# A streaming gradient: stores on their own DMA queue, loads issued one by one

## The chip, the cores and the metric

The kernel runs on one core of a Trainium2 chip. The metric is the device time of one execution in microseconds (us), taken as the median of several runs. Durations inside the kernel come from one profiled execution, recorded by the hardware profiler.

## The reference

```python
def setup_inputs():
    return {"x": np.random.randn(8192, 8192).astype(np.float32)}

def reference(x):
    return np.gradient(x, axis=1)
```

Along each row of 8192 numbers, an inner element of the result is half the difference of its two neighbours, `(x[j+1] - x[j-1]) / 2`; the first and last are the one-sided differences `x[1] - x[0]` and `x[8191] - x[8190]`. Input and output are 268.44 MB each, and there is nothing to reuse between rows.

## The kernel before

**Tiles.** The 8192 rows are cut into 32 sets of 256 rows. In a set each of the 128 partitions holds two whole rows side by side (`R = 2`), so a partition's piece is 16,384 numbers, 65,536 bytes, in one contiguous run of memory. Sets 0 to 2 are *plain*: partition p holds row pair p of the set. All others are *dealt*: the row pairs are given out to the partitions as cards are, so that partition 4a + q holds row pair 32q + a. Load and store of a set use the same order; the result of the computation does not depend on it.

**Slots.** Three buffers (`slot0` to `slot2`, `NB = 3`) take the sets in turn; set i uses slot i mod 3. A slot is 64 elements wider than a set. The load writes it from element 64 on (`SH = 64`), and VectorE writes the halved differences to the same buffer from element 1 on, in place but shifted, so that it overwrites only what it has already read.

**A set's work.** First GpSimd (POOL) computes the four one-sided differences per partition into `ends` (line 73). Then one custom VectorE (DVE) instruction does all the halved differences of the set, across the border between the two rows as well (line 79). Then the four end values are copied from `ends` over the wrong ones (line 90), by POOL in 12 of the sets and by DVE in the other 20. Then the store is issued (line 63). TensorE and ScalarE (ACT) do no work.

**Order.** All is written out by hand under `tc.manual_schedule()`. `chain` names for each step what it has to wait for: the end differences for the load, DVE for the end differences, the copy for DVE, the store for the copy, and load i for store i - 3, which empties its slot. Both loads (line 59) and stores (line 63) are issued by SyncE (SP), so they share one DMA queue, and its order is that of the program: three loads, three stores, three loads, three stores and so on, with two and two at the end. After the store of every third set come the loads of the next three:

```python
            if i % NB == NB - 1:
                for k in range(i + 1, min(i + 1 + NB, nsets)):
                    load(k)
```

Of the kernel before, what the change touches and what calls it, by code (L numbers as in the profile page):

```python
# [1 line left out]

# [4 lines left out]


@with_exitstack
def kernel(  # L10
    ctx: ExitStack,
    tc: tile.TileContext,
    x: bass.AP,
    out: bass.AP,
):

    nc = tc.nc
    P = nc.NUM_PARTITIONS
    n, m = x.shape
    R = 2  # L20
    NB = 3
    SH = 64
    W = R * m
    nsets = n // (P * R)
    f32 = x.dtype

    Q = 4

    def sets(t):

        plain = t.rearrange("(s p t) m -> s p (t m)", p=P, t=R)
        dealt = t.rearrange("(s q a t) m -> s a q (t m)", q=Q, a=P // Q, t=R)
        return [plain[i] if i < NB else dealt[i] for i in range(nsets)]

    x_sets, out_sets = sets(x), sets(out)

    pool = ctx.enter_context(tc.tile_pool(name="pool", bufs=1))
    edge = 256 // 4
    nends = nsets * R * 2
    ends_pad = pool.tile([P, nends + edge // 2], f32, name="ends", tag="ends")  # L40
    ends = ends_pad[:, 0:nends].rearrange("p (s t e) -> p s t e", t=R, e=2)
    slots = [pool.tile([P, SH + W], f32, name=f"slot{k}", tag=f"slot{k}") for k in range(NB)]
    loads, stores = [], [None] * nsets
    in_front = {}

    def chain(i, ins, *needed):

        group, engine = f"slot{i % NB}", ins.ins.engine
        keep = [o.ins for o in needed]
        if in_front.get(engine, (None,))[0] == group:  # L50
            keep.append(in_front[engine][1])
        tc.declare_no_dep(ins.ins, group=group, keep=keep, reason="implied by the needed step")
        tc.add_to_no_dep_group(group, ins.ins)
        in_front[engine] = group, ins.ins
        return ins

    def load(i):
        b = slots[i % NB]
        ins = nc.sync.dma_start(out=b[:, SH : SH + W], in_=x_sets[i])  # L59
        loads.append(chain(i, ins, *([stores[i - NB]] if i >= NB else [])))  # L60

    def store(i, done):
        ins = nc.sync.dma_start(out=out_sets[i], in_=slots[i % NB][:, 0:W])
        stores[i] = chain(i, ins, done)

    with tc.manual_schedule():
        for i in range(NB):
            load(i)
        for i in range(nsets):
            b = slots[i % NB]  # L70
            xin = b[:, SH : SH + W].rearrange("p (t m) -> p t m", m=m)

            ins = nc.gpsimd.tensor_sub(  # L73
                out=ends[:, i, :, :],
                in0=xin[:, :, 1 : m : m - 2],
                in1=xin[:, :, 0 : m - 1 : m - 2],
            )
            at = [chain(i, ins, loads[i])]
            ins = nc.vector._custom_dve(  # L79
                dve_ops.TENSOR_TENSOR_REDUCE_SUB_MAX,  # L80
                out=b[:, 1 : W - 1],
                in0=b[:, SH + 2 : SH + W],
                in1=b[:, SH : SH + W - 2],
                s0=0.0,
                s1=0.5,
            )
            halved = chain(i, ins, *at)
            res = b[:, 0:W].rearrange("p (t m) -> p t m", m=m)
            placer = nc.gpsimd if i % 5 in (1, 3) and i < nsets - 2 else nc.vector
            ins = placer.tensor_copy(out=res[:, :, 0 : m : m - 1], in_=ends[:, i, :, :])  # L90
            placed = chain(i, ins, halved)
            store(i, placed)
            if i % NB == NB - 1:
                for k in range(i + 1, min(i + 1 + NB, nsets)):
                    load(k)


# [1 line left out]
_INS = ['x']  # L99
_OUTS = [((8192, 8192), 'float32')]  # L100


# [23 lines left out]
```

## Time and profile before

| | |
|---|---|
| median of 3 runs | 1245.82 us (1245.79 to 1246.45) |
| the profiled execution | 1245.77 us, with a span of 1243.8 us |
| VectorE busy | 554.6 us (45%), 32 large instructions of 17.224 us each |
| GpSimd busy | 8.9 us (1%) |
| DMA | 536.88 MB on one queue, mean 432 GB/s, 9217 packets |
| loads, issue to landing | 32, median 57.9 us |
| stores, issue to landing | 32, median 40.3 us |

The span is the time from the first to the last recorded work of the profiled execution; its own time is 2.0 us longer. Engine rows give busy time and its share of the span. The slices of the page divide the span into 40 equal parts. A DMA row counts the packets that 16 DMA engines moved: 64 transfers, each with 128 packets of data (one for each partition) and 16 small ones that count the completion. "Issue to landing" runs from the issue of a transfer by SP until its last completion arrives, and so includes the time that it stands in the queue behind earlier transfers. SPq is the sequencer of SP that issues the transfers.

### The profile page before, as it was taken

To read this page: it belongs to the slowest core of one execution; us is meant where nothing else is said; L and a number is where in the kernel's file an instruction comes from. 1 tells how busy PE (TensorE), PEld (TensorE's weight loads), DVE (VectorE), ACT (ScalarE), POOL (GpSimd) and SP (SyncE) were. 2 spreads that over 40 slices of the span, in tenths; PEclk is the share of its full clock that TensorE was granted. 3 is DMA by queue.
4 is the path that set the end of the run, shared out by engine and by line. 5 is a ranking of instruction groups with operands and counts; after the bars stand their busy time and mean duration, and the time that the engine had idled before them with its cause. 6 is when DMAs were issued, how large, how long until landed. Compare 5 with 4: busy or idle time off the path is not lost.

```text
span 1243.8 us, 237 instructions
## 1 busy us (share of the span) xinstructions
DVE 554.6 (45%) x52; POOL 8.9 (1%) x48
## 2 busy tenths in 40 slices
DVE  2850583079009702850582079009603840591082
POOL 0000000000000000000000000000000000000000
DMA  9999999999999999999999999999999999999999
GB/s 405 438 438 424 419 438 438 438 438 426 434 430 430 438 438 438 426 438 432 430 432 438 438 430 434 438 432 430 432 438 434 434 434 438 432 430 430 436 409 405
DMA packets 9217, 536.88 MB, mean 432 GB/s; under 512 B 1024, under 2 KB 1024, under 8 KB 1024
## 3 DMA queue, kind: packets, MB, share of 16 engines
q1 hardware_dynamic: 9216, 536.88, 99.8%
q14 instruction: 1, 0.01, 0.0%
HBM read 268.44 MB, written 268.44 MB: 432 GB/s over the span
## 4 chain that ended last, share of the span: by engine, by line
another core or an unknown queue 74%; DVE 18%; DMA 3%; issue 2%; POOL 1%; SPq 0%; POOLq 0%
DVE slot L79 18%; DMA slot<-in_x_dram 3%; POOL ends L73 0%; POOL slot L90 0%; SPq L59 0%; POOLq L121 0%; DVE slot L90 0%
## 5 line engine op out<-in xcount | busy, mean ns | idle before, releaser
L79 DVE CUSTOM_DVE_ANT_0 slot<-slot 128x16382 f32<-128x16382 f32 x32 | 551.2, 17224 | 666.6 <-POOL ends L73 666.6
L73 POOL TENSOR_TENSOR ends<-slot 128x4 f32<-128x4 f32 x32 | 6.4, 200 | 987.4 <-DMA slot<-in_x_dram 987.4
L90 POOL COPY slot<-ends 128x4 f32<-128x4 f32 x12 | 2.3, 191 | 207.9 <-DVE slot L79 207.9
L90 DVE COPY slot<-ends 128x4 f32<-128x4 f32 x20 | 3.4, 172 | 0.7
L110 POOL MEMSET const-bfloat16-1.0<- 128x1 bf16 x1 | 0.1, 102 | 0.0
L110 POOL MEMSET const-uint8-127<- 128x1 uint8 x1 | 0.1, 102 | 0.0
L110 POOL MEMSET const-float32-0.0<- 128x1 f32 x1 | 0.1, 99 | 0.2 <-issue 0.2
L110 POOL MEMSET const-float32-1.0<- 128x1 f32 x1 | 0.1, 99 | 0.0
## 6 DMA issues: line engine op xcount, KB each, us to landing
slot<-in_x_dram SPq DMA_DIRECT2D x32, 57.9
out_dram<-slot SPq DMA_DIRECT2D x32, 40.3
```

Of the source, the lines that this page charges most:

```text
L73: ins = nc.gpsimd.tensor_sub(out=ends[:, i, :, :], in0=xin[:, :, 1 : m : m - 2], in1=xin[:, :, 0 : m - 1 : m - 2],)
L79: ins = nc.vector._custom_dve(dve_ops.TENSOR_TENSOR_REDUCE_SUB_MAX, out=b[:, 1 : W - 1], in0=b[:, SH + 2 : SH + W], in1=b[:, SH : SH + W - 2],
L90: ins = placer.tensor_copy(out=res[:, :, 0 : m : m - 1], in_=ends[:, i, :, :])
L110: nc = _bacc.Bacc("TRN2", target_bir_lowering=False, num_devices=1)
```

## The change

The stores are issued by ScalarE (`nc.scalar`) and so stand in a DMA queue of their own. The loads stay on SP. The load of set i + 3 is written right behind the store of set i, instead of three loads together behind every third store; its wait, for the store that empties its slot, is the same. Tiles, slots, layout and the computation are as before.

```diff
     def store(i, done):
-        ins = nc.sync.dma_start(out=out_sets[i], in_=slots[i % NB][:, 0:W])
+        ins = nc.scalar.dma_start(out=out_sets[i], in_=slots[i % NB][:, 0:W])
         stores[i] = chain(i, ins, done)
...
             store(i, placed)
-            if i % NB == NB - 1:
-                for k in range(i + 1, min(i + 1 + NB, nsets)):
-                    load(k)
+            if i + NB < nsets:
+                load(i + NB)
```

## The prediction

> **What bounds the kernel now.** I read the page's engine table and its slices first, then the DMA queues, then windows inside single phases, then the queue's own waits and the end of the chain.
>
> ```profile
> span 1243.8 us, 237 instructions
> ...
> DVE 554.6 (45%) x52; POOL 8.9 (1%) x48
> ...
> DMA  9999999999999999999999999999999999999999
> GB/s 405 438 438 424 419 438 438 438 438 426 434 430 430 438 438 438 426 438 432 430 432 438 438 430 434 438 432 430 432 438 434 434 434 438 432 430 430 436 409 405
> ...
> q1 hardware_dynamic: 9216, 536.88, 99.8%
> ```
>
> No slice has the DMA engines under nine tenths, and their one queue fills 99.8% of them; VectorE works 45% of the span. The kernel is bound by its transfers, so the question is whether the same bytes go through the 16 engines any slower or faster in another order. The windows, with columns DVE busy, POOL busy, granted TensorE clock, DMA share and GB/s, put one phase of stores and loads (80 to 138) beside one of loads and their computation (138 to 196) and the stores after it:
>
> ```profile
> 80.00:138.00 58.00, 0.00 (x0) 0.00 (x0) 1.00 1.00 434
> 138.00:196.00 58.00, 51.86 (x5) 0.79 (x4) 1.00 1.00 434
> 196.00:254.00 58.00, 0.15 (x1) 0.00 (x0) 1.00 1.00 434
> ```
>
> The rate is 434 GB/s whether VectorE works or not, and in both directions. The packet records say why: a packet of 65,536 B, one partition's row, takes 2,418 ns in 7,870 of 8,192 records and never under 2,415. Each engine moves 512 of them, 512 x 2.418 = 1,238.0 us. That is the floor, and the span is 5.8 us above it. For the slowest engine the 5.8 are: 1.8 until the first packet starts, 0.7 lost in the first packets, 1.0 where the first loads turn to the first stores (57 to 61 us), 1.6 over the other 20 turns and at the end, 0.8 after the last landing (rounded).
>
> ```profile
> SPq L63 <- DVE slot L90: 520.3, 20, 55.7
> SPq L59 <- DMA out_dram<-slot: 366.3, 29, 19.0
> SPq L63 <- POOL slot L90: 296.5, 12, 36.5
> ```
>
> These are the waits of SP's own queue. They are long, but they cost nothing: while SP waits for a store to land, two more stores are already queued on the engines.
>
> **What goes and what comes.** The profiled run took 1,245.77 us, its span 1,243.8; 2.0 lie outside the span and stay. The median of the runs is 1,245.82, so one more 0.05 is nothing.
>
> *Issue.* 32 stores leave SP for ACT, which has no other work. An issue takes 0.59 us on its sequencer (32 x 0.59 = 19 us per queue), all beside running transfers: 0. SP's load i+3 now waits for store i with no store behind it on SP; ACT's store i waits for set i's last copy, with only later stores behind it, which need later sets. DVE and POOL keep their order, in which POOL's end differences for set i+1 stand behind its copy for set i in 12 sets. Sets now arrive every 2 x 19.34 = 38.7 us, and landing to store issue takes 17.7 (22.69 to 40.38), so that wait is over 21 us before the next set lands: 0. The loads and stores still take turns on eight completion semaphores, but each user's predecessor is four sets older in its own direction, long landed: 0.
>
> *Do the engines ever run dry?* Stepping it through: loads 0 and 1 land as before; store 0 is issued at 40.4 and shares the engines with load 2, both done near 80. Store 1 has been queued since 59.5. Load 3 is issued at the landing of store 0 (in the present trace that takes 0.01 us at 81.6) and its first packet follows 1.0 us later (0.73 to 1.76 for load 0); for that long the load side is empty and store 1 has the engines alone. From then on one load and one store share, 38.7 us for each pair; every next store is issued 17.7 us after its load landed, so it stands ready 21 us early. Engines dry: 0. If that cover were gone, 29 reloads would each cost that 1.0 us and the landing's skew of up to 2.6 us, which is the rival below.
>
> *The end.* Now:
>
> ```profile
> 1184.91 0.20 POOL L73 TENSOR_TENSOR ends<-slot 128x4 f32<-128x4 f32 x1 [77.07 <-DMA slot<-in_x_dram]
> ...
> 1202.60 19.89 SPq L63 DMA_DIRECT2D out_dram<-slot  x2
> 1204.21 0.20 POOL L73 TENSOR_TENSOR ends<-slot 128x4 f32<-128x4 f32 x1 [19.10 <-DMA slot<-in_x_dram]
> ```
>
> Store 30 is issued at 1202.60 and needs 1.0 us to start; the slowest engine ends load 31 at 1204.14, so 0.3 is lost on it (it lands store 30 19.6 us later, not 19.3). After the change store 30 is ready long before: -0.3. But store 30 has then had the engines to itself about 1 us ahead of load 31, has 18.3 us left when load 31 lands, and store 31 starts 17.7 + 1.0 = 18.7 us after that landing: +0.4.
>
> *Turns.* This is the term that decides. The 21 turns between directions fall away: 1.3 of the 1.6 us is saved; the first turn's 1.0 stays, since loads still meet stores for the first time in the plain sets. In exchange load and store packets alternate on every engine. No second data queue exists in this trace, so the price of one alternation has to be bounded by the turns that it does show. Averaged over the 16 engines, the packets around a turn from loads to stores take too long by 984 ns at the first, then 140, 184, 84, 98, 0, 11, 7, 53 and 80; stores to loads 19, 5, 53, 0, 17, 4, 0, 5, 11 and 0. Early on the 16 engines turn within 0.5 us of each other, later within 1.6 to 2.6 us. Under two queues their turns are scattered, so the late ones are nearest: 30 + 6 = 36 ns for a pair from 580 us on. The bounds: 0 (three of the five last pairs are at 4 to 12 ns), and 84 ns, the mean over all but the first. Packets alternate from store 0's start to load 31's end, about 240 pairs per engine: 240 x 36 ns = +8.6 us, between 0 and 20.2.
>
> Here two rules of the skill bear. The Trainium skill, "DMA: Bandwidth & Descriptors", section "Queues, rings and completion order", says that an engine changes between queues only at packet boundaries, and that a packet typically holds 9 to 17 descriptors. A transfer here is 9,216 / 64 / 16 = 9 records per engine, so by that rule a whole transfer might be one turn: some 30 pairs, 30 x 84 = 2.5 us at the dearer price; no run here shows it yet. The same page of the Trainium skill, "Latency and other measured facts", gives 214 GB/s per direction as the full rate of a copy issued on the sync and scalar queues; by an estimate from that figure 536.88 MB / 428 GB/s = 1,254 us, which speaks against this change, while this trace's one queue shows 434.
>
> **Sum.** 1,243.8 - 1.3 - 0.3 + 0.4 + 8.6 = 1,251.2, and 2.0 outside: 1,253.2 us, slower by 0.6%.
>
> **Rivals.** A measurement of this kernel can tell about 0.2%, 2.5 us, from no change; slower begins at 1,248.3. With -1.2 from the other terms that takes 3.7 us in 240 pairs: 15 ns a pair.
>
> *No price for alternating (not slower).* The mechanism is that an engine fetches the next packet, of whichever queue, while it drains the present one. For it: three of the last five pairs below 15 ns, and 2,418 ns in all phases, so the engine and not the memory sets the rate. Against it: 64 and 80 ns in the two other pairs, and that no turn before 500 us was free in the direction load to store. Time: 1,253.2 - 8.6 = 1,244.6; with turns by whole transfers 1,247.1. It decides below 15 ns a pair.
>
> *Faster by over 0.2%.* The slowest engine has only 2.6 us to give (1.0 + 1.6): 1,243.2, which needs a free first turn, no price at all and no gap at the end. More would need packets under 2,418 ns, loads and stores overlapping inside an engine; no record is under 2,415 even at turns.
>
> *Lasting contention.* If reads and writes side by side in memory cost every packet what they cost in the first turns of the dealt sets (mean of 140, 184, 84 and of 19, 5, 53: 136 + 26 = 162 ns a pair), 240 x 162 = 39 us: 1,283. Against it: the price fell as the engines drifted apart.
>
> *The queues run dry.* If one queue took most of the engines, a store could end before the next is ready: up to 29 x (1.0 + 2.6) = 104 us, some 50 at half of it, 1,295. Against it: 21 us of slack.
>
> *The change doesn't do what it says.* SP's loads could still queue behind something. The order on each engine shows loads alone on SP and stores alone on ACT: no chance of its own.
>
> **Chances.** Alternation at 15 to 84 ns a pair 0.43 (1,248.3 to 1,264.8), lasting contention 0.05, dry queues 0.03: slower 0.51. No price, or whole transfers 0.42: same. Faster 0.07. Both signs hold much, so the likeliest case's own range is 1,248 to 1,265. The whole range is 1,243 to 1,268: from the slowest engine's full gain to a little past the dearest late price, leaving out the two dear rivals and half of faster.
>
> **What would show it.** Right: two hardware queues of 268 MB each; DMA share still at 99% or more; packets of loads and stores spread above 2,418 ns by some 18 ns on average; windows of 58 us at about 431 GB/s instead of 434; DVE waiting about 21 us for each set, evenly. If packets stay at 2,418 and the share at 99.8%, alternation is free and I am wrong by the 8.6. If packets exceed 2,500 throughout, it is contention. If the DMA share drops below 98%, a queue ran dry; POOL's waits for loads would then name it. If packets fall below 2,415, the floor was not one.

## The result and the profile after

The changed kernel is slower: 12 runs between 1,248.72 and 1,276.78 us, beside 1,245.42 to 1,246.80 for the kernel before. The ratio of the times is 1.0085, with a 95% interval of 1.0062 to 1.0108, or 1,256.4 us against 1,245.86. That ratio takes the eight runs within 1.5% of the fastest and leaves out four of 1,269 to 1,277 us, with which the median of the twelve is 1,261.6. The spread is a result by itself: 28 us where the kernel before has 1.4.

The profiled run took 1,250.96 us. These are the page's totals, slices and queues of the kernel after:

```profile
span 1248.6 us, 264 instructions
...
DVE 554.6 (44%) x52; POOL 8.9 (1%) x48
...
DMA  9999999999999999999999999999999999999997
GB/s 403 435 437 437 437 435 422 424 433 435 437 433 430 435 437 437 437 437 437 430 428 428 437 430 435 435 437 437 437 437 437 437 437 428 424 435 433 433 435 319
...
q1 hardware_dynamic: 4608, 268.44, 49.8%
q10 hardware_dynamic: 4608, 268.44, 49.6%
```

There are two queues of 268 MB now, and the engines are as busy as before in all slices but the last, where the rate drops to 319 GB/s. The windows of the kernel after (columns DVE busy, POOL busy, granted TensorE clock, DMA share, GB/s) put the middle beside the end:

```profile
600.00:658.00 58.00, 25.94 (x3) 0.39 (x2) 1.00 1.01 436
1100.00:1158.00 58.00, 28.32 (x3) 0.39 (x2) 1.00 1.00 435
1206.00:1228.00 22.00, 17.40 (x2) 0.20 (x1) 1.00 0.76 331
1228.00:1249.00 21.00, 0.00 (x0) 0.00 (x0) 1.00 0.83 359
```

Loads and stores mixed run at 435 GB/s, no less than in phases. The loss lies at 1,206 to 1,228 us, while VectorE computes the last set. In the kernel before the engines were full while it did (a window counts whole packets, so its share can pass 1.00):

```profile
1206.00:1222.00 16.00, 15.84 (x2) 0.00 (x0) 1.00 1.06 459
```

SP issues only loads now, and its waits are for the stores that empty their slots:

```profile
SPq L59 <- DMA out_dram<-slot: 1143.6, 29, 80.2
```

The end of the timeline of the kernel after gives the times:

```profile
1170.38 0.20 POOL L73 TENSOR_TENSOR ends<-slot 128x4 f32<-128x4 f32 x1 [38.18 <-DMA slot<-in_x_dram]
...
1208.98 0.20 POOL L73 TENSOR_TENSOR ends<-slot 128x4 f32<-128x4 f32 x1 [38.41 <-DMA slot<-in_x_dram]
1209.22 17.22 DVE L79 CUSTOM_DVE_ANT_0 slot<-slot 128x16382 f32<-128x16382 f32 x1 [21.18 <-POOL ends L73]
1226.48 0.17 DVE L90 COPY slot<-ends 128x4 f32<-128x4 f32 x1
```

Load 31 has landed on all engines at 1,208.9 us, 4.8 later than before (1,204.1), and its store can be issued at 1,226.7 only. By the packet records store 30 is over at 1,221.9 on the median engine and 1,223.4 on the last.

**An account for each run.** Linking each packet to the one that starts as it ends splits the records into 16 engines. A packet starts 4 ns ahead of its predecessor's recorded end, so 512 packets take 512 x 2.414 = 1,236.0 us. What lies between the first packet and the last beyond that is either the slowest engine's gaps in the last 100 us or time lost in slow packets. (The gap is the smallest over the engines. Where slow packets overlap, a few links go to the wrong engine; the sums here do not hang on that.) For the runs with packets of 32,768 B the floor is 1,024 x 1.209 = 1,238.0.

```
                first to last   lost by the     gap at      spread of the
                   packet      slowest engine   the end   landings of load 31
before            1240.9            4.9           0.1            2.5
after             1245.6            4.8           4.8            2.6
again_a           1267.0           26.2           4.9           20.0
again_b           1255.6           14.8           4.9           14.4
again_c           1255.5           14.7           4.8           17.3
swapped           1262.4           21.6           4.8           18.0
plain_all         1250.1           12.0           2.1            7.3
half              1249.5            8.7           4.9            6.5
hold_s30          1242.3            4.4           2.0            1.8
r1_two            1242.0            4.0           0.0       2.1 (last load)
r1_two_nb3        1246.2            4.5           3.7       1.8 (last load)
r1_one            1243.2            5.2           0.0       2.5 (last load)
```

The last column is the time from the first to the last of the 16 engines' landings, in us. In the first profile after, the gap at the end is the whole difference. In the longer runs one engine loses 10 to 21 us more.

### The profile page after: what moved, and what is told of

The parts are those of the page before. It is cut to its first block, busy times and chain, and to the rows that moved or that the text cites. A ratio compares the mean times of both kernels' runs of the same rounds, so it can differ in the third digit from the quotient of the medians.

```text
span 1248.6 us, 264 instructions
## 1 busy us (share of the span) xinstructions
DVE 554.6 (44%) x52; POOL 8.9 (1%) x48
## 2 busy tenths in 40 slices
DMA packets 9216, 536.88 MB, mean 430 GB/s; under 512 B 1024, under 2 KB 1024, under 8 KB 1024
## 4 chain that ended last, share of the span: by engine, by line
another core or an unknown queue 82%; DMA 9%; issue 3%; DVE 3%; SPq 1%; POOL 0%; POOLq 0%
DMA slot<-in_x_dram 5%; DMA out_dram<-slot 3%; DVE slot L79 3%; SPq L59 1%; POOL ends L73 0%; DVE slot L90 0%; POOLq L120 0%
```

## The experiments

**The kernel again, and the end by itself.** `again_a`, `again_b` and, on another occasion, `again_c` are the changed kernel unaltered.

> The changed kernel once more, unaltered, since its runs lie between 1248.7 and 1276.8 us while those of before lie within 1.4 us. Theory E (the end): the profile of after shows 8,192 packets at 2,418 ns almost throughout and a gap of some 5.7 us between the last packets of store 30 and the first of store 31; the runs differ in how far the stores lead the loads when load 31 lands, so a longer run has a longer gap there, 0.4 to some 20 us, and its middle stays at 434 GB/s. Theory C (contention): in a longer run the packets in the middle take longer, 20 us of excess being 40 ns per packet, a mean of about 2,458 ns instead of 2,423, and the gap at the end stays near 5.7 us. Theory D (dry queues): the DMA share of windows in the middle falls to 0.98 with packets at 2,418.

> The changed kernel unaltered a third time, for one more profile. Theory E: span less 1,242.9 us equals the gap between stores 30 and 31, packets at 2,418 ns. Theory C: the gap stays at 5.7 us and the excess of the packets over 2,418 ns, summed and divided by 16 engines, makes up the rest. Theory D: share in the middle below 0.985.

Measured: `again_a` 1,263.0 to 1,276.5 us (4 runs, median 1,269.1, ratio 1.0189, 1.0145 to 1.0233; the profile's span 1,269.9), `again_b` 1,260.5 (span 1,258.6). The gap on the slowest engine is 4.9 us in both, so theory E does not explain the spread. Theory C fails as written, too: the mean packets of `again_b` are 2,434 ns for loads and 2,418 for stores, an excess of 8 ns over all, 4 us per engine, while the span is 10 us longer than that of the first profile. The excess sits on one or two engines. Over 2,418 ns a packet, fourteen of the sixteen engines of `again_b` lost 2 to 6 us each, the other two about 14; those two land store 30 at 1,233.1 and 1,233.4 us, the others by 1,225.7. The windows of `again_a` show what that does at the end:

```profile
1100.00:1158.00 58.00, 24.19 (x2) 0.58 (x3) 1.00 0.99 416
1212.00:1231.00 19.00, 0.40 (x1) 0.20 (x1) 1.00 0.90 390
1231.00:1250.00 19.00, 16.99 (x2) 0.00 (x0) 1.00 0.17 72
1250.00:1270.00 20.00, 0.00 (x0) 0.00 (x0) 1.00 0.85 367
```

From 1,231 to 1,250 us nearly all engines stand still (share 0.17). Fifteen have ended store 30 and wait for the last set, which could not be computed before the straggler's share of load 31 had landed. From 1,100 to 1,158 us of this run, at 416 GB/s, the lag is about 20 us, nearly the 21 us by which a store is ready early. From 900 to 1,200 us the stores' packets average 2,486 to 2,513 ns, and 56% of all time lost in packets is in first packets of stores. That would fit a store queue that now and then runs dry as a consequence of the lag, but theory D is not shown by it: the share is 0.99, not 0.98, and from 100 to 1,200 us no engine stands idle for more than 2.6 us in all.

```diff
+    def sides(i):
...
+            if i < nsets - 1:
+                at = [sides(i)]
+            else:
+                at = [last_sides]
...
-            placer = nc.gpsimd if i % 5 in (1, 3) and i < nsets - 2 else nc.vector
+            if i == nsets - 2:
+                last_sides = sides(nsets - 1)
+            placer = nc.gpsimd if (i % 5 in (1, 3) and i < nsets - 2) or i == nsets - 2 else nc.vector
```

`sides(i)` issues the end differences of set i. Those of set 31 now stand ahead of set 30's copy, both on GpSimd.

> The changed kernel, but store 30 is held until load 31 has landed: GpSimd takes the end differences of set 31 ahead of the copy that releases store 30. Nothing else moves. Theory E: load 31 no longer shares the engines with store 30, lands some 4 us earlier, and store 30 covers the computation of set 31 in full; the gap ahead of store 31 falls from 5.7 to under 1 us, a gap of 1 to 3 us comes instead between load 31 and store 30, and the profiled span falls by 2 to 4 us against a run of the changed kernel with the same middle; if the end makes the spread, the runs also draw together, to within 3 us. Theory C: the gap at the end falls likewise, but the runs still spread over more than 10 us.

The timeline of `hold_s30` at the end, with POOL's differences of set 31 at 1,203.65 (`sides`) and the issues of stores 30 and 31, the first at 1,204.01, the second done 17.88 us later:

```profile
1203.65 0.20 POOL L68 TENSOR_TENSOR ends<-slot 128x4 f32<-128x4 f32 x1 [33.57 <-DMA slot<-in_x_dram]
...
1204.01 17.88 ACTq L63 DMA_DIRECT2D out_dram<-slot  x2
1221.14 0.17 DVE L97 COPY slot<-ends 128x4 f32<-128x4 f32 x1
```

Two windows of `hold_s30` show the engines before store 30 and beside it, while VectorE computes the last set:

```profile
1196.00:1206.00 10.00, 2.11 (x1) 0.32 (x2) 1.00 0.76 328
1206.00:1225.00 19.00, 15.28 (x2) 0.00 (x0) 1.00 1.02 442
```

Load 31 lands 5.3 us earlier than in the profile after, the gap ahead of store 31 is gone, one of 2.0 stands between load 31 and store 30, and the span is 1,245.3 instead of 1,248.6: 3.3 us less, where theory E names 2 to 4. Still the ten runs reach from 1,246.1 to 1,267.3 (ratio 1.0054, 1.0025 to 1.0083). The gap and the straggler are two losses.

**The order alone, on one queue.**

```diff
-        ins = nc.scalar.dma_start(out=out_sets[i], in_=slots[i % NB][:, 0:W])
+        ins = nc.sync.dma_start(out=out_sets[i], in_=slots[i % NB][:, 0:W])
```

> The order of the changed kernel (store i, then load i + 3) with all transfers on SP, so that the stores have no queue of their own. Load i + 3 waits for the landing of store i at the head of the queue, and store i + 1, long ready, stands behind it. Both theories: at each landing the engines are empty for the 1.0 us from issue to first packet and the skew of the landing, 29 times 1.5 to 3 us, so 1,290 to 1,330 us, a DMA share of 93 to 97%. If it is near 1,246 instead, the second queue is not what keeps the engines supplied.

Measured: 1,367.0 us (one run), more than expected. SP's waits (in total, times, longest), and one window of `one_queue`:

```profile
SPq L59 <- DMA out_dram<-slot: 1206.4, 29, 42.1
```

```profile
600.00:658.00 58.00, 17.40 (x2) 0.20 (x1) 1.00 0.95 398
```

Each of the 29 reloads waits at the head with the next store behind it, and the engines run empty: 121 us more than before are 4.2 us for each; of them 75 us (5.5% of the span) show as idle engines and the rest as slow packets: behind each wait every engine has two of some 3.3 us instead of 2.4. The landings stay within 1.4 us of each other, for the engines meet at every wait. So the new order is affordable only with the second queue; what the second queue adds is the subject of the rest.

**Where the straggler comes from.**

> The changed kernel unaltered, as the measure for the other three on the same chip. Theory G (a straggler): one or a few of the 16 engines lose some hundred ns in a load packet now and then, most often in the first packet of the next load, and as every engine has its own fixed 512 packets nothing gives the time back; the span is that of the slowest engine, 1,243 us plus its lost time beyond 2 us, plus the gap of some 5 us at the end. The landings of a late load are then spread over as many us as the span is above 1,248 (2.6 us at 1,248.6, 14 at 1,258.6, 20 at 1,269.9 so far). Rival C (contention of all engines alike): the spread stays under 5 us whatever the span.

Measured: 1,250.2 to 1,272.6 us (7 runs), span 1,258.4, spread of load 31's landings 17.3 us, 14.7 us lost. It fits theory G in kind, since rival C had the spread under 5 us; its size was to be 10, the span less 1,248. In the packets of this run about 71% of all lost time after the first 100 us lies in the first packet of a load; in the other profiles of full-size sets with dealt tiles whose stores do not wait it is 34% (after), 57% (`again_b`) and 84% (`hold_s30`). These shares are good to some 7 points, as the linking of slow packets is.

```diff
-        return [plain[i] if i < NB else dealt[i] for i in range(nsets)]
+        return [plain[i] for i in range(nsets)]
```

> The changed kernel with all 32 sets plain, none dealt. If the straggler's lost time comes from where in memory the engines read and write at one time, the layout changes it: a first turn among plain sets cost the kernel before 1.0 us per engine, one among dealt sets 0.14, so a straggler might lose several times as much, 1,290 us and over, or all engines lose alike. If it comes from the alternation of two queues in itself, the times lie in the range of the changed kernel, 1,248 to 1,277 us.

Measured: 1,254.9 to 1,270.1 us (4 runs, ratio 1.0113, 1.0064 to 1.0163), 12.0 us lost by the slowest engine. So the dealt layout is not what makes the straggler.

```diff
-        ins = nc.sync.dma_start(out=b[:, SH : SH + W], in_=x_sets[i])
+        ins = nc.scalar.dma_start(out=b[:, SH : SH + W], in_=x_sets[i])
...
-        ins = nc.scalar.dma_start(out=out_sets[i], in_=slots[i % NB][:, 0:W])
+        ins = nc.sync.dma_start(out=out_sets[i], in_=slots[i % NB][:, 0:W])
```

> The changed kernel with the two queues exchanged: loads on ACT, stores on SP. The slow packets of the changed kernel are loads (mean 2,434 against 2,418 ns for stores in the run of 1,258.6 us). If that is a matter of direction, loads stay the slow ones, now on the other queue, and times lie between 1,248 and 1,277 us. If it is a matter of which queue an engine serves first, the stores become the slow ones.

Measured: 1,250.9 to 1,267.9 us (4 runs; the profile's span 1,265.4). From 200 to 400 us loads average 2,433 ns and stores 2,418, as before the exchange: there the slow packets follow the direction. Past 400 us the lag is 18 us, and the stores' first packets wait as in `again_a`; over the whole run the stores average 2,438 ns and the loads 2,432. So the direction is shown for the first 400 us only.

```diff
-        ins = nc.sync.dma_start(out=b[:, SH : SH + W], in_=x_sets[i])
...
+        for h in range(2):
+            n = x_sets[i].shape[0] // 2
+            ins = nc.sync.dma_start(
+                out=b[h * P // 2 : (h + 1) * P // 2, SH : SH + W], in_=x_sets[i][h * n : (h + 1) * n]
+            )
...
```

Only the loads are shown; the stores are halved likewise.

> The changed kernel with each load and each store issued as two transfers of 64 partitions: per engine the same 512 packets of 65,536 B and about the same number of alternations, but twice as many transfer ends and first packets. If the straggler's time is lost at the first packets of loads, it has twice the occasions: the excess and the spread double on average, median near 1,280 us. If it is lost per alternation wherever that falls, nothing changes: 1,248 to 1,277 us.

Measured: 1,706.7 to 1,758.9 us (4 runs), which answers another question than the one asked. The engines do not rest, but their packets are slow; a window of `halves`:

```profile
1000.00:1058.00 58.00, 17.40 (x2) 0.20 (x1) 1.00 1.00 302
```

Packets of the same 65,536 B take 4.0 us as loads and 2.7 as stores on average. Why is not shown, and whether more first packets make more lag can't be read from it.

```diff
+    half = 15
...
-        ins = nc.scalar.dma_start(out=out_sets[i], in_=slots[i % NB][:, 0:W])
+        queue = nc.sync if i < half else nc.scalar
+        ins = queue.dma_start(out=out_sets[i], in_=slots[i % NB][:, 0:W])
...
-            if i + NB < nsets:
+            if i < half and i % NB == NB - 1:
+                for k in range(i + 1, i + 1 + NB):
+                    load(k)
+            if i >= half and i + NB < nsets:
                 load(i + NB)
```

> Both kernels in one: sets 0 to 14 as before (one queue, three loads, three stores), from set 15 on the stores on ACT and each load behind the store of its slot. Theory G: the landings of the first half lie within 1.5 us of each other, as before; from some 620 us on the spread grows by the rates seen so far (2 to 20 us in 1,200 us), to 2 to 10 us, and the gap at the end is the same 5 us: 1,248 to 1,262 us, a median near 1,254. If the lag grows from the start, or the second half shows none, alternation is not its cause.

Measured: 1,251.1 to 1,261.7 us (7 runs, median 1,251.3, ratio 1.0061, 1.0038 to 1.0084). The landings stay within 1.5 us until 622 us, the end of the old order; with the second queue they are 3.1 us apart for loads at 705, 4.3 at 936 and 6.5 at 1,207. The kernel before has 1.7 us at 643 and 2.6 at 1,204, so within one execution the lag grows faster behind the change. Queue and order change together at set 15. In `one_queue`, the order alone, no lag builds up, but there the engines meet at every wait.

**Depth or size.**

```diff
-    R = 2
-    NB = 3
+    R = 1
+    NB = 6
```

> The changed kernel with one row per partition and set (R = 1) and six slots: the same bytes in 64 sets, packets of 32,768 B, a VectorE instruction of some 8.6 us, and two or more loads always queued ahead. Theory G with the loss in the alternation itself: twice as many first packets of loads, so the straggler loses 10 to 50 us and the times spread from 1,250 to 1,290; only the gap at the end halves, from 5 to some 2.5 us. Rival H (the loss comes from a load queue that is only one transfer deep, so that its next first packet is late): with several loads queued the first packets start at once, the spread of the landings stays under 3 us, and the median is 1,244 to 1,249.

> The kernel before, with the same smaller sets (R = 1, six slots, six loads, then six stores, one queue): the control for r1_two. With 64 more completions of next to nothing and the same 21 turns it should stay within 0.2% of before, 1,243.5 to 1,248, spread of landings under 3 us, all runs within 2 us. If it is slower by more, smaller packets cost something by themselves and r1_two has to be read against it.

Measured: `r1_two` 1,246.66 to 1,247.76 us in ten runs, `r1_one` 1,247.39 to 1,248.96. Against the kernel before the ratios are 1.0009 (0.9999 to 1.0018) and 1.0018 (1.0008 to 1.0027): no version beats it, and two queues are no slower than one here. The small sets cost 2 us by themselves (the two floors, 1,238.0 against 1,236.0). In `r1_two` the straggler is gone (spread of landings at most 2.1 us) and so is the gap. On the same chip `half`, with full-size sets, had it. Queues, waits of SP and windows at the end of `r1_two`:

```profile
q1 hardware_dynamic: 9216, 268.44, 50.1%
q10 hardware_dynamic: 9216, 268.44, 49.9%
```

```profile
SPq L59 <- DMA slot<-in_x_dram: 773.9, 59, 19.5
SPq L59 <- DMA out_dram<-slot: 340.1, 58, 6.3
```

```profile
1205.00:1228.00 23.00, 12.50 (x3) 0.20 (x1) 1.00 1.00 432
1228.00:1239.00 11.00, 3.15 (x2) 0.00 (x0) 1.00 1.01 438
```

The engines work at full rate until 1,239 us, 6 us before the end. SP waits mostly for the fourth load back, since four of the eight completion semaphores serve the loads in turn: 71.3 us from issue to landing are almost four of the 19.4 us that a pair takes, so several loads are always queued. That agreed with rival H, but the size had changed along with the depth. The last run keeps the size and takes the depth back (`NB = 3`):

> The small sets on two queues (R = 1, packets of 32,768 B) with three slots instead of six, so that again only one load is on its way while the next waits for its store: all sizes of the changed kernel halved, its depth kept. Rival H (depth): the slow first packets and the straggler come back, landings spread over 4 to 20 us late in the run, the gap at the end is some 2 to 5 us, and the median lies at 1,250 to 1,290 us with runs more than 5 us apart. Rival P (size: packets of 32,768 B are what kept r1_two even): as r1_two, spread near 2 us, packets at 1,213 ns, 1,247 to 1,250 us with runs within 2 us.

Measured: 1,250.42 to 1,251.10 us in five runs (ratio 1.0039, 1.0024 to 1.0053).

```profile
SPq L59 <- DMA out_dram<-slot: 1164.6, 61, 41.0
```

```profile
1205.00:1228.00 23.00, 8.90 (x3) 0.39 (x2) 1.00 1.00 433
1228.00:1239.00 11.00, 8.82 (x2) 0.00 (x0) 1.00 0.53 229
```

SP waits for stores alone again, as in the kernel after, and the gap at the end is back: half the engines' time from 1,228 to 1,239 us. But the straggler is not: spread of landings 0.8 to 2.9 us after the first hundred, median packets at 1,213 ns, runs within 0.7 us. Rival H falls for the straggler, though the gap of 3.7 us is the one that it names; rival P holds for the straggler, though its time of 1,247 to 1,250 us is missed, by that gap. In these runs, then, **depth decides the gap, and the size of the sets decides the straggler**. Two limits: full-size sets were never run deeper than three slots, and `r1_two_nb3` ran on a chip (7) on which the changed kernel did not; the straggler is there on the three chips (0, 3 and 9) on which two queues with full-size sets were run for the experiments. Theory G, too, was wrong to expect twice the loss with twice the first packets.

Open: whether it is the packet of 65,536 B, the transfer of 8.4 MB or the time between first packets, and what in an engine makes its first load packet wait when it runs behind the others. No run here changes one of these alone.

## Why the prediction was right, and where it was not

The direction and the size hold: 1,253.2 us forecast, 1,256.4 measured, within 1,248 to 1,265. That the size came out is luck. The largest term of the sum, 8.6 us for alternating, is not there; a gap of 4.8 us, of which the sum has 0.4, and a straggler, which it does not have, come to about as much. Three of the four runs of `again_a` lie above 1,265.

- *The bound.* Right: 434 to 436 GB/s in the middle of the kernel after, DVE waiting 21 us for each set. The floor was 2.0 us too high, because records overlap by 4 ns.
- *Issue: 0.* Right: store 0 has landed at 82.31 us, and load 3 is issued at 82.33.
- *Engines dry: 0.* Right in the first profile. But the stores' lead over the loads was put at about 1 us of work, and that is the error behind the next point. The first packets of load 3 start at 86.8 to 88.3 us, 4.5 to 6.0 behind its issue and not 1.0, and stores have had the engines to themselves since load 2 landed (78.7 on the median engine). The landings of the median engine settle with stores 9 us ahead of loads (store 29 at 1,197.7, load 31 at 1,206.7). A load also lands a turn behind its data: the last data packets of load 31 end at 1,203.6 to 1,206.2, and on each engine one more store packet runs before the small one that counts the load.
- *The end: -0.3 + 0.4.* The mis-sized term: the gap measured 4.8 us on the slowest engine. The wait of 17.7 + 1.0 us was right, but store 30 had some 14 us left to cover it instead of 18.3. `hold_s30` took 3.3 us of span back.
- *Turns: -1.3 + 8.6.* The step that failed. Alternation was free in the profile after: 7,879 of 8,192 packets take 2,418 ns, the stores average 2,418.2 ns, the loads 2,428.5, most of whose excess lies in the first 300 us, and the slowest engine lost 4.8 us as against 4.9 before. That is the prediction's own sign of being wrong by the 8.6, and the 1.3 us that fewer turns were to save does not show either. So rival *no price for alternating* described the mechanism of this profile; its time of 1,244.6 was short by the gap. The late turns of the one queue were not the row to read. Load and store packets take turns one by one on every engine, but for the ends of transfers: about 210 changes from load to store per engine, where the prediction counted 240, so the pairs were nearly right and their price was not there. The Trainium skill, "DMA: Bandwidth & Descriptors", section "Queues, rings and completion order", has engines changing queues at packet boundaries. The trace agrees, if one packet is one record of 65,536 B; turns by the nine records of a transfer it does not show. By an estimate from the 214 GB/s per direction that the same page of the Trainium skill gives under "Latency and other measured facts" for copies between HBM tensors, two queues would have reached 428 GB/s; the windows show 435, and the measurement decides.
- *Lasting contention.* It was priced at 39 us, for all engines alike. What came is narrower and smaller: in the longer profiles of the changed kernel one engine loses 10 to 21 us more than in the kernel before, and all wait for it at the end.

Together: 4.8 to 4.9 us of gap in all four profiles of the changed kernel, and 0 to 21 us of straggler, which differs from run to run.

## What to carry to other kernels

Read a transfer-bound kernel by its slowest DMA engine, not by the mean rate: every engine has a fixed share of each transfer, and the spread of a transfer's 16 landings shows a straggler that 99% busy engines hide. When loads and stores share the engines, ask at the end of the kernel what is still queued while the last set is computed; in these runs more depth (with small sets) or a store held back gave that time back, all or most of it. Where runs of one kernel spread more than its neighbour's, one profile is not enough.

## What the runs showed of the hardware that was not expected

- With loads and stores on two queues in packets of 65,536 B, single engines fall behind by up to 23 us within one execution (`again_a`, the stores at 1,141 us); with 32,768 B the same pattern stays within 3 us.
- A straggler's lag grows in steps and rests between them: in `again_b` the spread of the loads that land from 518 to 712 us is 7.1 to 7.8 us (3 x 2.414 = 7.2), of those from 907 to 1,101 it is 12.1 to 12.7 (5 x 2.414 = 12.1). That the rests are whole packets is not shown: in `swapped` it is 17.7 to 18.2 us from 642 us on, 7.4 packets.
- A load's last data packet and the small packet that counts it are a turn apart on two queues: in the profile after, 2.4 us with a store packet between them.
- Transfers over 64 partitions reach 302 to 320 GB/s in windows where those over 128 reach 434.
